# The recurrent mixer's three levels of scores as 32-column blocks in one group of matmuls

## The chip, the cores and the metric

The kernel runs on one core of a Trainium2 chip. The metric is device time in microseconds (us); one execution is one launch of the whole program. TensorE (PE in the profile) does the matmuls, its weight loads stand apart as PEld; VectorE is DVE, ScalarE is ACT, GpSimd is POOL, SyncE (SP) starts most transfers.

## The reference, cut to what matters

The reference is an encoder trunk of two layers over 1024 tokens of width 1024. Layer 0 mixes tokens by windowed attention, layer 1 by a gated linear recurrence that runs over the sequence in both directions; each mixer has four cross-attention heads beside it, and a ConvGLU follows each mixer. The change touches the recurrence alone:

```python
def gla_chunked(q, k, v, log_f):            # per head: 128 keys, 128 values
    b = jnp.cumsum(log_f, axis=2)           # within a chunk
    q_dec = q * jnp.exp(b)
    k_dec = k * jnp.exp(-b)
    s = jnp.where(causal, jnp.einsum('bcthk,bcshk->bchts', q_dec, k_dec), 0.0)
    o_intra = jnp.einsum('bchts,bcshv->bcthv', s, v)
    ...                                     # plus q_dec times a state carried from chunk to chunk
```

Scores `s` are wanted between tokens of one chunk, for the forward direction where the key is not later than the query, for the backward direction where it is not earlier.

## The kernel before, in words

The kernel works in chunks of 128 tokens. A call of `direction` handles one head `h`, one direction `d` and one half `b` of the sequence, so 512 tokens or four chunks; there are 8 heads x 2 directions x 2 halves = 32 such calls, in the order (0,0), (1,1), (0,1), (1,0) of (d, b) within a head. Everything in it is laid out as 128 keys (partitions) by 512 tokens.

**The scores of one call.** A bank of PSUM, `pa`, holds 4 chunks of 128 x 128 scores, the key's token on the partition and the query's token in the column. To keep the exponentials in range they are made at three levels:

- level 16: `E1` (queries) and `E2` (keys), scaled relative to the middle of each block of 32 tokens; L1116 multiplies them as one full 128 x 128 product for each chunk;
- level 32: one tile `G` whose earlier or later halves of 32 tokens hold scaled keys and scaled queries; L1136 multiplies, for each chunk, two blocks of 32 x 32 off the diagonal, over the product of level 16;
- level 64: a second `G`, and L1136 puts one block of 64 x 64 in each chunk.

Between the levels `step` (L1122, L1123) carries the decays `EP` and `ER` to the next block size; half of each `G` is made by POOL (L1130), half by DVE (L1131). Then a masked copy on DVE (L1146) takes only the wanted triangle out of `pa` into a zeroed tile `Az`, which goes to `As`. Beside it `ER` is transposed (`pt`, L1155), copied to `kT` by ACT (L1157) and multiplied with the values (`pu`, L1160) to carry the state.

**Buffers.** `E1`, `E2`, both `G`, and the four scratch tiles before them (`a_`, `L1`, `R`, `B`) rotate through five buffers with the tag `E`, eight allocations a call. So `L1` of the next call, written by the second activation (L1082), is put into the buffer of this call's `E1`, and may be written when the level-16 product has read it. `pa` rotates through two banks, which the cross-attention's scores `ps` share; `pt` has two banks, `pu`, `po` one each, and `pj`, the projections, two.

**What sets the order.** The projections of the next head (`proj`, three matmuls of 512 columns for each product: L81, L82, L83), the cross-attention units and the output products (`po`, L1184) are independent work that fills TensorE between the steps of a call. Nobody writes that order out: a scheduler runs the program against its own table of costs when it is built and fixes the order of each engine's queue. On the chip each queue then runs strictly in that order and waits for semaphores. `issue_after(x)` forbids the scheduler to place the instructions under it ahead of `x`.

The float32 matmuls that aren't split into high and low parts (`pa`, `pu`, `po`) appear in the trace as two passes each, with a weight load for each pass: the 128 matmuls of L1116 are 256 rows. A transpose is one pass.

Of the kernel before, what the change touches and what calls it, by code (L numbers as in the profile page):

```python
# [6 lines left out]
F32 = mybir.dt.float32  # L7
# [9 lines left out]
P = 128  # L17
# [29 lines left out]
def build(tc, A, out):  # L47
    nc = tc.nc
    act, dve, pool, pe = nc.scalar, nc.vector, nc.gpsimd, nc.tensor
# [889 lines left out]
    def hgrn():  # L939
# [5 lines left out]
        V, G = [late.tile([P, 3, NT, P], F32, name=x) for x in ("v", "gs")]  # L945
        wp = tc.alloc_tile_pool(name="hg1", bufs=1, side="right", reuse_waits="tile")
        psp = tc.alloc_tile_pool(name="hgps", bufs=1, space=PSUM, side="right", reuse_waits="tile")
        psj = tc.alloc_tile_pool(name="hgpj", bufs=2, space=PSUM, reuse_waits="tile")
        PB = dict(pa=2, pt=2, pu=1, po=1)

        def bank(tag, shape=(P, 4, P)):
            return psp.tile(list(shape), F32, tag=tag, bufs=PB[tag], name=tag)

        class Bank:
            tile = staticmethod(lambda shape, dt, tag, bufs, name: psp.tile(shape, dt, tag=tag, bufs=bufs, name=name))

        tags = {"pj": ("pj", 2, psj), "ps": ("pa", 2, Bank), "pt": ("pt", 2, Bank), "po": [lambda x=x: bank(x, (P, 512)) for x in ("po", "pu")], "sm": 1, "xo": "ot"}
        one = lambda shape, name, dt=F32: wp.tile(shape, dt, bufs=1, name=name)
        for x in PB:
            bank(x)  # L960
        lg = one([P, 2, 2, 8], "lg")
        nc.sync.dma_start(lg, A["lb_logits"])
        bng = one([P, 8], "bng")
# [102 lines left out]
        def direction(h, r, d, b, qin, S, As):  # L1066
# [3 lines left out]
            lt, er = (0, 1) if d else (1, 0)  # L1070

            def E():
                return early.tile([P, 512], F32, tag="E", bufs=5, name="E")

            def halves(x, n):
                x = x.rearrange("p (b a c) -> p b a c", a=2, c=n)
                return x[:, :, lt, :], x[:, :, er, :]
# [16 lines left out]
            ER = early.tile([P, 512], F32, tag="ER", bufs=2, name="ER")  # L1094
            act.activation(EP, B, AF.Exp)
            act.activation(ER, R, AF.Exp)
            pa = bank("pa")
            E1, E2 = E(), E()
            Bl, Be = halves(B, 16)
            Rl, Re = halves(R, 16)  # L1100
# [3 lines left out]
            def parts(n):  # L1104
                return halves(EP, n) + halves(ER, n) + halves(q, n) + halves(k, n)
# [5 lines left out]
            dve.tensor_tensor(e2, re_, ke, op=ALU.mult)  # L1111
            dve.tensor_tensor(e1, e1, qe, op=ALU.mult)
            dve.tensor_tensor(l2, l2, kl, op=ALU.mult)
            for c in range(4):
                cs = slice(c * P, (c + 1) * P)
                pe.matmul(pa[:, c, :], E2[:, cs], E1[:, cs], start=True, stop=True)  # L1116

            def step(n):
                pl_, pe_, rl_, re_ = parts(n)[:4]
                e = 0 if d else n - 1  # L1120
                nb = 512 // (2 * n)
                dve.tensor_tensor(re_, re_, bc(pl_[:, :, e:e + 1], [P, nb, n]), op=ALU.mult)  # L1122
                dve.tensor_tensor(pl_, pl_, bc(pe_[:, :, e:e + 1], [P, nb, n]), op=ALU.mult)  # L1123

            for n in (32, 64):
                step(n // 2)
                G = E()
                gl, ge = halves(G, n)
                pl_, pe_, rl_, re_, ql, qe, kl, ke = parts(n)
                pool.tensor_tensor(gl, pl_, ql, op=ALU.mult)  # L1130
                dve.tensor_tensor(ge, re_, ke, op=ALU.mult)  # L1131
                for c in range(4):
                    for i in range(64 // n):
                        o = i * 2 * n
                        lo, eo = o + lt * n, o + er * n
                        pe.matmul(pa[eo:eo + n, c, lo:lo + n], G[:, c * P + eo:c * P + eo + n],  # L1136
                                  G[:, c * P + lo:c * P + lo + n], start=True, stop=True,
                                  tile_position=(0, eo))
            step(64)
            dec = wp.tile([P, 4], F32, tag="dec", bufs=2, name="dec")  # L1140
            e = 0 if d else P - 1
# [16 lines left out]
            pu = bank("pu")  # L1158
# [54 lines left out]
        def head(h, r):  # L1213
            qin = [wp.tile([P, T], F32, tag=f"qin{d}", bufs=1, name="qin") for d in range(2)]
            S = [wp.tile([P, NT, P], F32, tag=f"S{d}", bufs=1, name="S") for d in range(2)]
            As = [None, None]
            for i, (d, b) in enumerate(((0, 0), (1, 1), (0, 1), (1, 0))):
                direction(h, r, d, b, qin[d], S[d], As)
                if i < len(r["later"]):
                    r["run"](r["later"][i])  # L1220
                cross(HX[h][i])
                if h == 7 and i == 2:
                    wo1.early(psj, 2, es)
            if h == 7:
                early.release()
                es.release()
                eq.release()
                wo1.open(2, 0)
            for i, b in enumerate((1, 0)):
                output(h, r, b, qin, S, As)  # L1230
                cross(HX[h][4 + i])
# [44 lines left out]
    wo0.finish()  # L1276
    ffn(0, wo0, h2d, True, (0, 1), (0, 1))
    hgrn()
    wo1.finish()
    ffn(1, wo1, out, False, (1, 0), (1, 0))  # L1280
# [83 lines left out]
```

## Time and profile before

| what | value |
|---|---|
| median of 3 runs (lowest to highest) | 2722.17 us (2719.72 to 2722.46) |
| span of the profiled execution, first to last instruction | 2718.9 us |
| TensorE busy over the span | 2656.1 us (98%) |
| DVE, ACT, POOL busy | 1830.8, 1396.6, 472.8 us |
| mean granted clock of TensorE | 0.993 |
| recurrent stage | about 1250 to 1950 us of the span |

How to read it: a row of the timeline gives the start, the time from the first start to the last end, and `xN` passes merged. Matmuls overlap in the pipeline, so what a matmul costs is read from the distance between starts, not from its own duration. In a shape such as `128*32` the second number is how many columns of the array the instruction uses, and `128x32` is the output columns that it streams.

### The profile page before, as it was taken

What the parts mean: (1) busy time and instruction counts of PE and PEld (TensorE: products, weight loads), DVE (VectorE), ACT (ScalarE), POOL (GpSimd) and SP (SyncE); (2) the same over time, 40 slices, a digit from 0 to 9 for tenths busy, and PEclk for the clock granted to TensorE, in tenths of its full rate; (3) what the DMA queues carried; (4) which work ended last, traced back from release to release, by engine and by line L of the source; (5) the groups of instructions that cost most, each with busy time, mean ns of one, the idle gap of its engine ahead of it and who ended that gap; (6) DMA issues with size and microseconds to landing.
All of it is one profiled execution on the core that took longest, in us unless ns stands there. A gap on an engine that the chain in (4) does not pass through costs nothing.

```text
span 2718.9 us, 37473 instructions
## 1 busy us (share of the span) xinstructions
PE 2656.1 (98%) x13472; PEld 2228.1 (82%) x13472; DVE 1830.8 (67%) x3040; ACT 1396.6 (51%) x2556; POOL 472.8 (17%) x520
## 2 busy tenths in 40 slices
PE   8899999999999999999999999999999999999998
PEld 7888897788888887887888888888788788888887
DVE  6487787678565655478686777868567756566447
ACT  6367667545444444454444545545454544444443
POOL 1231110211111100032232231312121111110003
PEclk9899999999999999999999999999999999999999
DMA  7674213667777757573234541111466787775766
GB/s 283 204 167 101 59 37 113 183 192 182 205 198 199 201 149 259 191 250 132 80 131 113 117 93 55 44 54 37 124 213 178 187 212 200 203 198 153 233 195 233
DMA packets 215307, 432.12 MB, mean 159 GB/s; under 512 B 20560, under 2 KB 77264, under 8 KB 209488
## 3 DMA queue, kind: packets, MB, share of 16 engines
q1 hardware_dynamic: 188128, 335.07, 38.3%
q0 software_dynamic: 24544, 90.19, 16.0%
q10 hardware_dynamic: 2448, 4.46, 0.5%
q8 instruction: 106, 1.74, 0.3%
q14 instruction: 81, 0.66, 0.1%
HBM read 335.79 MB, written 117.96 MB: 167 GB/s over the span
## 4 chain that ended last, share of the span: by engine, by line
PE 89%; DVE 6%; ACT 2%; DMA 2%; issue 1%; SPq 0%; POOL 0%; DVEq 0%; POOLq 0%; ACTq 0%
PE X L535 29%; PE V L535 11%; PE pj L81 8%; PE pj L82 7%; PE pj L83 7%; PE Y L535 5%; PE pb L81 3%; PE pb L82 3%; PE pb L83 3%; PE po L1184 1%; PE pa L1136 1%; PE pt L116 1%; PE pt L338 1%; PE pa L1116 1%; PE pu L1160 1%
## 5 line engine op out<-in xcount | busy, mean ns | idle before, releaser
L87 DVE TENSOR_TENSOR wl<-st,wh 128x1024 fp32r<-128x1024 f32 (+1 forms) x238 | 262.2, 1109 | 326.7 <-ACT wh L86 323.0
L86 ACT CAST wh<-st 128x1024 fp32r<-128x1024 f32 (+1 forms) x238 | 222.5, 937 | 295.4 <-PE X L535 195.9
L81 PE MATMUL pj<-uh,wh 128*128 128x512 f32 x512 | 206.9, 404 | 6.6 <-DVE xl L87 4.6
L535 PE MATMUL X<-wl,wh 128*128 128x512 f32 x528 | 204.7, 389 | 0.0
L535 PE MATMUL X<-wh,wl 128*128 128x512 f32 x528 | 204.6, 389 | 0.0
L82 PE MATMUL pj<-ul,wh 128*128 128x512 f32 x512 | 203.2, 397 | 0.1
L83 PE MATMUL pj<-uh,wl 128*128 128x512 f32 x512 | 203.2, 397 | 0.0
L535 PE MATMUL X<-wh 128*128 128x512 f32 x528 | 198.8, 390 | 1.3 <-ACT c L908 1.3
L81 PE MATMUL pj<-wh,uh 128*128 128x384 f32 (+1 forms) x512 | 191.4, 374 | 0.0
L82 PE MATMUL pj<-wl,uh 128*128 128x384 f32 (+1 forms) x512 | 187.5, 366 | 0.0
L83 PE MATMUL pj<-wh,ul 128*128 128x384 f32 (+1 forms) x512 | 187.1, 365 | 0.0
L535 PE MATMUL V<-uh,wh 128*128 128x512 f32 x344 | 133.8, 389 | 0.0
L535 PE MATMUL V<-ul,wh 128*128 128x512 f32 x344 | 133.8, 389 | 0.0
L535 PE MATMUL V<-uh,wl 128*128 128x512 f32 x344 | 133.8, 389 | 0.0
L77 DVE TENSOR_TENSOR wl<-st,wh 128x1024 fp32r<-128x1024 f32 (+1 forms) x92 | 113.3, 1239 | 27.1 <-ACT wh L76 26.2
L76 ACT CAST wh<-st 128x1024 fp32r<-128x1024 f32 (+1 forms) x99 | 99.8, 1014 | 47.1 <-PE pj L82 27.2
L81 PEld LDWEIGHTS pj<-uh,wh 128*128 128x128 f32 x512 | 97.2, 190 | 26.9 <-DVE xl L87 5.5
L1130 POOL TENSOR_TENSOR E<-EP,q 128x256 f32<-128x256 f32 x64 | 54.6, 854 | 371.6 <-DVE EP L1123 286.5
L535 PEld LDWEIGHTS X<-wh 128*128 128x128 f32 x528 | 99.1, 188 | 22.7 <-ACT c L908 1.7
L535 PEld LDWEIGHTS X<-wh,wl 128*128 128x128 f32 x528 | 99.1, 188 | 20.7
L535 PEld LDWEIGHTS X<-wl,wh 128*128 128x128 f32 x528 | 99.1, 188 | 20.4
L83 PEld LDWEIGHTS pj<-uh,wl 128*128 128x128 f32 x512 | 97.4, 190 | 19.7
(348 smaller groups left out, 7336.1 us busy)
## 6 DMA issues: line engine op xcount, KB each, us to landing
st<-hid SPq DMA_DIRECT2D x154, 256.0 KB, 3.2
st<-in_ffw_dram SPq DMA_DIRECT2D x108, 256.0 KB, 3.3
w2s<-in_ffw_dram POOLq DMA_DIRECT2D x24, 1024.0 KB, 7.9
st<-in_ffw_dram SPq DMA_DIRECT2D x46, 512.0 KB, 3.8
hid<-tt SPq DMA_DIRECT2D x88, 256.0 KB, 4.7
st<-w2s SPq DMA_DIRECT2D x88, 256.0 KB, 3.2
sx<-in_ffw_dram SPq DMA_DIRECT2D x84, 256.0 KB, 4.0
sy<-in_ffw_dram SPq DMA_DIRECT2D x42, 512.0 KB, 6.0
```

The costliest lines, as they stand in the source:

```text
L76: act.copy(h[:, :n], raw)
L77: (eng or dve).tensor_tensor(l[:, :n], raw, h[:, :n].bitcast(F32), op=ALU.subtract)
L81: pe.matmul(o, ah, bh, start=first, stop=False)
L82: pe.matmul(o, ah, bl, start=False, stop=False)
L83: pe.matmul(o, al, bh, start=False, stop=last)
L86: act.copy(h, src)
L87: dve.tensor_tensor(l, src, h.bitcast(F32), op=ALU.subtract)
L116: pe.transpose(ps[:, k, :], u[:, (4 * b + k) * P:(4 * b + k + 1) * P], ident)
L338: pe.transpose(tp[:, j, :], sm[:, j, c * P:(c + 1) * P], ident)
L535: pe.matmul(o, x, y, start=new, stop=e, skip_group_check=not first)
L1116: pe.matmul(pa[:, c, :], E2[:, cs], E1[:, cs], start=True, stop=True)
L1130: pool.tensor_tensor(gl, pl_, ql, op=ALU.mult)
```

## The change

All three levels are cut so that each matmul uses 32 columns of the array: level 16 as the four 32 x 32 blocks on the diagonal of each chunk (it was one 128 x 128 product), level 32 as before, level 64 as two blocks of 32 x 64 for each chunk (it was one of 64 x 64). They are issued as one group behind the operand of the last level: first the eight blocks of level 64, then, held back by `issue_after`, the sixteen of level 16 and the eight of level 32. That is 32 matmuls a call where there were 4 + 8 + 4 = 16, over the whole kernel 1024 for 512.

Since the blocks don't cover the bank, `pa` is now one bank for each direction, set to zero once by DVE at the start of the mixer. The cross-attention's `ps` moves from the tag `pa` to the two banks of `pt`.

```diff
-        PB = dict(pa=2, pt=2, pu=1, po=1)
+        PB = dict(pt=2, pu=1, po=1)
...
-        tags = {"pj": ("pj", 2, psj), "ps": ("pa", 2, Bank), "pt": ("pt", 2, Bank), "po": [lambda x=x: bank(x, (P, 512)) for x in ("po", "pu")], "sm": 1, "xo": "ot"}
+        tags = {"pj": ("pj", 2, psj), "ps": ("pt", 2, Bank), "pt": ("pt", 2, Bank), "po": [lambda x=x: bank(x, (P, 512)) for x in ("po", "pu")], "sm": 1, "xo": "ot"}
...
+        PA = [psp.tile([P, 4, P], F32, tag=f"pa{d}", bufs=1, name="pa") for d in range(2)]
+        for x in PA:
+            dve.memset(x, 0.0)
...
-            pa = bank("pa")
+            pa = PA[d]
...
-            for c in range(4):
-                cs = slice(c * P, (c + 1) * P)
-                pe.matmul(pa[:, c, :], E2[:, cs], E1[:, cs], start=True, stop=True)
+            def block(c, i, j, x, y, n=32):
+
+                return pe.matmul(pa[i:i + 32, c, j:j + n], x[:, c * P + i:c * P + i + 32], y[:, c * P + j:c * P + j + n],
+                                 start=True, stop=True, tile_position=(0, i))
...
+                if n == 32:
+                    G32 = G
+            for c in range(4):
+                for o in (0, 32):
+                    mm = block(c, er * 64 + o, lt * 64, G, G, 64)
+            with tc.issue_after(mm.ins):
                 for c in range(4):
-                    for i in range(64 // n):
-                        o = i * 2 * n
-                        lo, eo = o + lt * n, o + er * n
-                        pe.matmul(pa[eo:eo + n, c, lo:lo + n], G[:, c * P + eo:c * P + eo + n],
-                                  G[:, c * P + lo:c * P + lo + n], start=True, stop=True,
-                                  tile_position=(0, eo))
+                    for o in range(0, P, 32):
+                        block(c, o, o, E2, E1)
+                for c in range(4):
+                    for o in (0, 64):
+                        block(c, o + er * 32, o + lt * 32, G32, G32)
```

In the changed file the lines of a call stand further down: `block` is L1119, the transposes of `ER` L1164, the state's product L1169, the output product L1193.

The order of the queues moves with it. TensorE, the fourth call of the first head, before: a call's scores between the state's product `pu` and the projections `pj`.

```order
L1160 MATMUL pu<-v,kT 128x128 x4
L1116 MATMUL pa<-E 128x128 x4
L1136 MATMUL pa<-E 32x32 x8
L1136 MATMUL pa<-E 64x64 x4
L83 MATMUL pj<-uh,wl 128x512
L81 MATMUL pj<-uh,wh 128x512
```

The fourth call of the first head now: `32x64` is level 64, the 24 blocks of `32x32` are levels 16 and 32.

```order
L1193 MATMUL po<-S,qin 128x128
L1119 MATMUL pa<-E 32x64 x8
L1119 MATMUL pa<-E 32x32 x24
L1164 MATMUL pt<-ident,ER 128x128 x4
L81 MATMUL pj<-uh,wh 128x512
L82 MATMUL pj<-ul,wh 128x512
```

Three shapes of the array in a row have become one. Counted over the whole queue, 32-column runs between other work are 73 now (19 calls have all 32 matmuls together, the other 13 are still cut into pieces); before, there were 82 runs of 32 or 64 columns, 57 of them entered from a 128-column matmul and 25 that are a 64-column run right behind a 32-column run.

TensorE, the second call of the second head, before: behind the scores come two projections, the transposes of `ER`, and 24 more projections ahead of the product `pu`.

```order
L1116 MATMUL pa<-E 128x128 x4
L1136 MATMUL pa<-E 32x32 x8
L1136 MATMUL pa<-E 64x64 x4
L83 MATMUL pj<-uh,wl 128x512
L81 MATMUL pj<-uh,wh 128x512
L1155 MATMUL pt<-ident,ER 128x128 x4
L82 MATMUL pj<-ul,wh 128x512
L83 MATMUL pj<-uh,wl 128x512
```

The same call now: the transposes, two projections, `pu`, and then 24 projections (the first three are shown) up to the next call's group.

```order
L1119 MATMUL pa<-E 32x64 x8
L1119 MATMUL pa<-E 32x32 x24
L1164 MATMUL pt<-ident,ER 128x128 x4
L82 MATMUL pj<-ul,wh 128x512
L83 MATMUL pj<-uh,wl 128x512
L1169 MATMUL pu<-v,kT 128x128 x4
L81 MATMUL pj<-uh,wh 128x512
L82 MATMUL pj<-ul,wh 128x512
L83 MATMUL pj<-uh,wl 128x512
```

The level-16 product, whose end lets the next call's L1082 start, has moved from ahead of the call's other scores to behind the level-64 blocks, and between it and the next call's first block stands only the work of these rows. Outside the recurrent stage TensorE's order is the same as before.

## The prediction

> **What bounds the kernel now.** I read the page's totals and chain first, then the busy times of the stage that changes, then what TensorE waits for in it.
>
> ```profile
> span 2718.9 us, 37473 instructions
> ...
> PE 2656.1 (98%) x13472; PEld 2228.1 (82%) x13472; DVE 1830.8 (67%) x3040; ACT 1396.6 (51%) x2556; POOL 472.8 (17%) x520
> ...
> PE 89%; DVE 6%; ACT 2%; DMA 2%; issue 1%; SPq 0%; POOL 0%; DVEq 0%; POOLq 0%; ACTq 0%
> ```
>
> ```profile
> 1250.00:1950.00 700.00, 688.00 (x4177) 576.34 (x4176) 521.37 (x1039) 352.95 (x771) 176.28 (x189) 1.00 0.29 83
> ```
>
> ```profile
> PE pj L81 <- DVE xl L87: 2.1, 1, 2.1
> PE po L1184 <- DVE S L1169: 2.1, 1, 2.1
> PE pt L217 <- DVE xp L212: 0.9, 2, 0.8
> PE pa L1116 <- ACT xp L208: 0.9, 2, 0.5
> ```
>
> TensorE is 98% busy and holds 89% of the chain that ended last. In the recurrent stage (columns: stretch, length, PE, PEld, DVE, ACT, POOL, then the granted clock, here 1.00) it is busy 688 of 700 us, DVE 521. The longest waits of TensorE there are about 2 us, and those for the scores under 1. So a microsecond that TensorE's queue loses here is one that the kernel loses, as long as no new wait takes its place.
>
> **What the scores cost on TensorE.** The rows grouped by shape, in the same stretch:
>
> ```profile
> L1116 PE MATMUL pa<-E 128*128 128x128 f32 x256 | 35.7, 276 | 1.3 <-ACT xp L208 0.9 <-DVE E L1113 0.3
> L1136 PE MATMUL pa<-E 128*64 128x64 f32 x256 | 22.6, 229 | 0.0
> L1136 PE MATMUL pa<-E 128*32 128x32 f32 x512 | 17.4, 200 | 0.0
> ```
>
> These durations overlap, so I don't add them; I take the distances of starts. One call in one piece, between projections:
>
> ```profile
> 1556.65 0.39 PE L83 MATMUL pj<-uh,wl 128*128 128x512 f32 x1
> 1556.88 1.05 PE L1116 MATMUL pa<-E 128*128 128x128 f32 x8
> 1557.86 1.05 PE L1136 MATMUL pa<-E 128*32 128x32 f32 x24
> 1558.85 0.50 PE L81 MATMUL pj<-uh,wh 128*128 128x512 f32 x1
> 1559.18 0.39 PE L82 MATMUL pj<-ul,wh 128*128 128x512 f32 x1
> 1559.41 0.40 PE L83 MATMUL pj<-uh,wl 128*128 128x512 f32 x1
> ```
>
> A projection takes 0.23 (1559.18 to 1559.41). From 1556.88 to 1559.18 are 2.30, with one projection in it: the call's scores cost **2.07 us**. The second L1136 row merges 16 passes of 32 columns and 8 of 64. The 32-column passes can be taken apart with four other places:
>
> ```profile
> 1277.20 0.39 PE L83 MATMUL pj<-uh,wl 128*128 128x512 f32 x1
> 1277.52 0.31 PE L1136 MATMUL pa<-E 128*32 128x32 f32 x6
> 1277.76 0.50 PE L81 MATMUL pj<-wh,uh 128*128 128x512 f32 x1
> 1278.10 0.39 PE L82 MATMUL pj<-wl,uh 128*128 128x512 f32 x1
> ...
> 1309.41 0.26 PE L1136 MATMUL pa<-E 128*32 128x32 f32 x4
> 1309.59 0.50 PE L81 MATMUL pj<-wh,uh 128*128 128x512 f32 x1
> ...
> 1397.83 0.45 PE L1136 MATMUL pa<-E 128*32 128x32 f32 x16
> 1398.20 0.50 PE L81 MATMUL pj<-uh,wh 128*128 128x512 f32 x1
> ...
> 1440.85 0.25 PE L1136 MATMUL pa<-E 128*32 128x32 f32 x2
> 1441.03 0.50 PE L81 MATMUL pj<-wh,uh 128*128 128x512 f32 x1
> ```
>
> From a run's start to the next start: one matmul (2 passes) 0.18, two 0.18, three 0.24, eight 0.37. The second matmul is free: it goes to another 32 columns of the array than the first (64 apart) and runs beside it. The third, alone with its columns, costs 0.06; two more pairs and a partner cost the rest. So a matmul of 32 x 32 occupies its 32 columns for 0.064 us, and two such column groups overlap fully: 0.032 a matmul, 0.016 a pass. Next, the price of changing shape: from 1277.20 to 1278.10 are 0.90, less two projections 0.44, less the bodies 0.064 + 0.064: **0.32 us for each run of narrow matmuls**, in and out. And the 64-column part: 0.99 (1557.86 to 1558.85) less 0.37 is 0.62, less the 0.12 that a run has beyond its body (0.37 - 8 x 0.032) 0.50, or 0.125 for each matmul that streams 64 columns.
>
> **Before, all calls:** 32 x 2.07 = 66.2. The queue has 57 runs entered from a wide matmul instead of 32, 25 x 0.32 = 8.0 more, and seven calls have no direct step from 32 to 64 columns, 7 x 0.12 = 0.8 less. Sum **73.4 us**.
>
> **Now, a call:** level 64: eight matmuls of 32 x 64 in two column groups, four rounds of 0.125 = 0.50, if neighbouring groups overlap as those 64 apart do. Level 32: eight of 32 x 32 in two groups, 0.26, as before. Level 16: sixteen over four groups. With four side by side 0.26, with two 0.51. No row shows four; I take 0.30, near the lower end, because the second group added less than 0.01 in the rows above. Entry and exit 0.32. Sum 1.38, times 32 is 44.2. There are 73 runs instead of 32: 41 x 0.32 = 13.1. Sum **57.3**, with level 16's ends 56.0 to 64.0. TensorE gains **16.1 us** (9.4 to 17.4).
>
> [...]
>
> **What is late next.** The level-16 product now ends last, and L1082 of the next call waits for its buffer. One call after such a release, to its last level-64 operand:
>
> ```profile
> 1545.34 0.63 ACT L1082 ACTIVATE E<-E 128x512 f32<-128x512 f32 x1
> ...
> 1555.26 0.76 POOL L1130 TENSOR_TENSOR E<-EP,q 128x256 f32<-128x256 f32 x1 [1.21 <-DVE EP L1123]
> ```
>
> ```profile
> 1471.66 0.63 ACT L1082 ACTIVATE E<-E 128x512 f32<-128x512 f32 x1 [4.23 <-PE pa L1116]
> ...
> 1486.91 0.79 POOL L1130 TENSOR_TENSOR E<-EP,q 128x256 f32<-128x256 f32 x1 [1.88 <-DVE EP L1123]
> ```
>
> The chain takes 10.7 us in the first, 16.0 in the second, where other work stands between its steps on ACT and DVE. Against that I hold the TensorE work that the new order puts from the end of level 16 to the next call's first block, priced by the distances above (a pass of 128 columns 0.11: eight in 1556.88 to 1557.86). It is 12.0 us or more at 30 of 31 places, 12.0 to 13.0 at twelve, and 15.9 at the call of the second row. One place is short, the second call of the second head: level 32 0.26, four transposes 0.44, 26 projections 5.9, `pu` 0.9, changes of shape 0.2: 7.7 us. There TensorE stands for 10.7 - 7.7 = **3 us**. At the other places the cover is over 1 us and I take 0.
>
> **The rest.** The two memsets on DVE, no row before:
>
> ```profile
> L988 POOL MEMSET Az<- 128x512 f32 x2 | 1.0, 526 | 0.0
> L1146 DVE COPY_PREDICATED Az<-gm,pa 128x512 f32<-128x512 uint8 x32 | 23.6, 736 | 7.7 <-PE pa L1136 7.5
> ```
>
> 0 to 1.5 us (two at 0.74); they lie under the first head's projections, 87 matmuls or 20 us ahead of the first score, so 0. The masked copy now waits for the whole group: it waited 7.5 us in all, behind it the next call's DVE steps; at most 0.8 us more (1.38 - 0.62) at the seven places where it already waits, 5 us; DVE has 179 us idle in the stage, so 0. The banks of `ps` come from `pt`, eight units: nothing if a transpose's bank is free, 0.9 each (row of L217 above) if not, 7 us; the order is built around it, so 0. Some of the 12 us that TensorE stands now may go, some come; 0, with 3 either way.
>
> **Sum.** 2718.9 - 16.1 + 3 = 2705.8 for the profiled execution, which lies 3.3 under the median of 2722.17: predicted **2709 us**.
>
> **The rivals.**
>
> *Two groups at a time.* Level 16 takes 0.51: 6.7 us more, 2716. For: two is all that the rows show. Against: nothing in them shows a limit.
>
> *A long train is fed too slowly.* The longest train of narrow passes so far is 24; now it is 64, and the queue ahead of TensorE may run dry. The gain is gone where 32 x (x + 0.32) + 13.1 = 73.4, so x = 1.56 us for 64 passes, 0.024 a pass. If all but the first 16 go at the mean of the 24-pass train, 0.99 / 24 = 0.041, a call takes 0.25 + 1.97 + 0.32 = 2.54, and the kernel 2746. Against: 16 passes at 0.016 without a sign of slowing. [...]
>
> *Neighbours don't overlap.* Level 64 now pairs adjacent column groups, which no row shows. If neighbours go one after the other, level 64 takes 1.00 and level 16 0.51: 0.71 x 32 = 23 more, 2732. With no overlap but that of level 32, level 16 takes 1.02: 2748.
>
> *The buffer of level 16 becomes the bound* (slower). The place is L1082, held until the group's end; the price is the chain less the cover. With a chain c everywhere the twelve places at about 12.7 and the short one eat the gain of 16.1 when 12 (c - 12.7) + (c - 7.7) = 16.1, c = 13.6. At c = 15 they take 35 us, 2741. For: 16.0 in the row above. Against: where the chain was that long, the new order has put 15.9 us of cover.
>
> *It doesn't do what it says.* One group a call is not what the queue has: 13 of 32 calls are still in pieces. That is in the sum (41 runs).
>
> **How the numbers follow.** Forecast 0.55 (2699 to 2713); two groups 0.13; slow feed 0.07; neighbours 0.10; the buffer 0.15, spread from 2715 up. The range of eight in ten is **2699 to 2732**: below, 2709 less 1.3 (level 16's end), 3 (no stall), 3 (old waits gone) and rounding; above, adjacent groups in turn. Past it lie half of the last two cases, the worst of the feed and a little below. A measurement of this kernel can tell about 0.2%, 5.4 us, from no change. Faster than 2716.7: the forecast and most of the two-group case, **0.65**. Within: the rest of that case, half of the slow feed, part of the buffer, **0.17**. Slower than 2727.6: neighbours, most of the buffer, half of the feed, **0.18**.
>
> **What would show it.** In the new profile: a whole group about 1.2 us from its first start to the start of what follows; 32-column passes of level 16 at 8 to 10 ns each; TensorE idle about 3 us ahead of one group in the second head; the stage some 13 us shorter. Wrong if a group takes over 2 us, or if TensorE waits at many groups for POOL or DVE.

## The result, and the profile after

The changed kernel takes **2718.07 us** (median of 12 runs, 2714.51 to 2723.15), the kernel before 2719.59 us on the same chips (median of 12, 2717.62 to 2722.88): ratio **0.9994**, 95% interval 0.9985 to 1.0002. It is no faster by any amount that the measurement can tell. The forecast was 2709.

First the page's totals, then the whole recurrent stage in one row for each kernel, from the same matmul to the same matmul. Columns: stretch, its length, then busy us (and instructions) of PE, PEld, DVE, ACT and POOL, then the granted clock, the DMA share and GB/s. Before:

```profile
1134.70:2056.10 921.40, 909.40 (x5193) 760.26 (x5192) 668.91 (x1239) 470.85 (x972) 230.16 (x234) 1.00 0.38 114
```

After:

```profile
span 2714.1 us, 39502 instructions
...
PE 2638.7 (97%) x14496; PEld 2204.5 (81%) x14496; DVE 1828.5 (67%) x3042; ACT 1391.6 (51%) x2556; POOL 468.4 (17%) x520
```

```profile
1131.60:2050.60 919.00, 896.70 (x6218) 740.83 (x6217) 665.39 (x1241) 466.58 (x972) 226.41 (x234) 0.99 0.38 115
```

The profiled span is 4.8 us shorter, but 3.1 of that lie ahead of the stage, where the programs are alike (it begins at 1131.6 for 1134.7), and 0.7 are lost behind it: the scatter of an execution. The stage itself is 2.4 us shorter: TensorE is busy 12.7 us less (909.4 to 896.7) and stands 10.3 us more (12.0 to 22.3). And the clock column says 0.99 where it said 1.00. That is no accident of the two profiles: the granted clock is 0.9914 on average over the 12 runs of the changed kernel, 0.9935 over 26 runs of the kernel before (those beside old_places), which is some 5.6 us more lost over the span.

**The group itself is as forecast.** TensorE at one of the cross units, after:

```profile
1660.09 0.39 PE L83 MATMUL pj<-uh,wl 128*128 128x512 f32 x1
1660.41 1.17 PE L1119 MATMUL pa<-E 128*32 128x64 f32 x64
1661.51 0.66 PE L1164 MATMUL pt<-ident,ER 128*128 128x128 f32 x4
1661.92 0.36 PE L81 MATMUL ps<-kvh,xh 128*128 128x256 f32 x1
...
1663.00 0.28 PE L83 MATMUL ps<-kvh,xl 128*128 128x256 f32 x1
1664.73 1.16 PE L1169 MATMUL pu<-v,kT 128*128 128x128 f32 x8 [1.45 <-ACT kT L1166]
1665.65 0.36 PE L81 MATMUL ps<-kvh,xh 128*128 128x256 f32 x1
```

All 64 passes of a call go in 1.10 us from first start to next start (1660.41 to 1661.51), where 1.2 was forecast. The last three rows show a new wait, to which the next part returns.

**Where TensorE stands now.** Five stretches of the stage, after:

```profile
1385.00:1410.00 25.00, 20.89 (x219) 16.90 (x218) 22.96 (x43) 13.76 (x25) 8.59 (x10) 1.00 0.46 153
...
1490.00:1500.00 10.00, 6.91 (x94) 5.68 (x93) 6.55 (x12) 6.49 (x15) 4.80 (x5) 0.86 0.83 190
...
1660.00:1670.00 10.00, 8.41 (x107) 6.98 (x106) 7.88 (x14) 7.38 (x16) 2.82 (x3) 1.00 0.06 20
...
1826.00:1832.00 6.00, 4.38 (x84) 3.47 (x83) 3.87 (x7) 4.29 (x9) 3.09 (x3) 0.98 0.20 74
...
1895.00:1947.00 52.00, 42.59 (x329) 33.88 (x327) 36.37 (x81) 24.07 (x65) 11.48 (x12) 0.90 0.38 114
```

The same places before; of the three cross units only one stood:

```profile
1390.00:1415.00 25.00, 23.64 (x162) 19.60 (x161) 24.10 (x45) 13.31 (x24) 8.54 (x11) 1.00 0.43 153
...
1835.00:1845.00 10.00, 7.86 (x40) 6.42 (x39) 9.90 (x24) 6.78 (x17) 1.06 (x2) 0.87 0.12 43
...
1900.00:1952.00 52.00, 45.77 (x296) 37.62 (x295) 37.59 (x84) 24.12 (x65) 11.42 (x12) 0.97 0.36 112
```

The second head: 4.1 us of idle for 1.4; here are two of its three waits.

```profile
1390.70 1.13 PE L1169 MATMUL pu<-v,kT 128*128 128x128 f32 x8 [0.97 <-DVE S L1178]
...
1398.98 1.17 PE L1119 MATMUL pa<-E 128*32 128x64 f32 x64 [1.44 <-DVE s L1041]
```

The second is the group that the prediction named: its last operand, POOL's half of `G`, is written from 1398.18 to 1398.93, though the label names `s`. The third wait, 1.7 for `q`, stood before too, with 1.4.

Three cross units: 3.1 + 1.6 + 1.6 = 6.3 for 2.1. The last head: 9.4 for 6.2. That is 10.1 of the 10.3. The waits by name, after (total us, times, longest):

```profile
PE pu L1169 <- ACT kT L1166: 4.4, 3, 1.5
PE pu L1169 <- ACT xo L223: 2.3, 1, 2.3
PE pb L81 <- ACT oh L86: 2.0, 2, 1.3
PE pb L83 <- DVE oe L87: 1.9, 1, 1.9
```

The first row was in no list of before. The others are steps of the last head, where few projections are left to lie over a wait.

**The second price of idle.** What follows the wait at 1494.78, after, by 2 us and then TensorE's rows:

```profile
1494.00:1496.00 2.00, 0.86 (x5) 0.66 (x5) 1.29 (x3) 2.00 (x5) 1.12 (x1) 1.00 0.92 188
1496.00:1498.00 2.00, 1.48 (x10) 1.48 (x11) 2.00 (x5) 1.70 (x3) 0.15 (x1) 0.81 1.01 201
1498.00:1500.00 2.00, 2.00 (x9) 1.81 (x9) 2.00 (x4) 1.59 (x6) 0.00 (x0) 0.50 0.96 197
1500.00:1502.00 2.00, 2.00 (x9) 1.61 (x8) 2.00 (x6) 1.19 (x3) 0.00 (x0) 0.83 1.10 229
```

```profile
1499.03 0.63 PE L81 MATMUL pj<-uh,wh 128*128 128x512 f32 x1
1499.46 0.63 PE L82 MATMUL pj<-ul,wh 128*128 128x512 f32 x1
1499.88 0.63 PE L83 MATMUL pj<-uh,wl 128*128 128x512 f32 x1
```

The granted clock falls to one half, and projections start 0.42 us apart, not 0.23 as at full clock. Such a stretch costs (0.19 + 0.50 + 0.17) x 2 = 1.7 us, and in it TensorE counts as busy. The stage before holds two, at 1842 and 1941, 3.4 us; after it holds five, at 1497, 1831, 1903 and two from 1930, 8.5 us.

So I count the stage in three parts: idle, the loss in half-clock stretches (sum of 1 - clock over windows of 1 us), and the rest, **work at full clock**. Before: 12.0 + 3.4 + 906.0. After: 22.3 + 8.5 + 888.2. TensorE was spared **17.8 us** of work, and 10.3 + 5.1 came back.

### The profile page after: what moved, and what is told of

Its sections match the earlier page's. It is cut to its first block, busy times and chain, and to the rows that moved or that the text cites. A ratio compares the mean times of both kernels' runs of the same rounds, so it can differ in the third digit from the quotient of the medians.

```text
span 2714.1 us, 39502 instructions
## 1 busy us (share of the span) xinstructions
PE 2638.7 (97%) x14496; PEld 2204.5 (81%) x14496; DVE 1828.5 (67%) x3042; ACT 1391.6 (51%) x2556; POOL 468.4 (17%) x520
## 5 line engine op out<-in xcount | busy, mean ns | idle before, releaser
L87 DVE TENSOR_TENSOR wl<-st,wh 128x1024 fp32r<-128x1024 f32 (+1 forms) x238 | 262.6, 1110 | 326.7 <-ACT wh L86 321.6
L77 DVE TENSOR_TENSOR wl<-st,wh 128x1024 fp32r<-128x1024 f32 (+1 forms) x92 | 119.0, 1301 | 23.3 <-ACT wh L76 22.8
```

The lines of the kernel that those rows point to most:

```text
L77: (eng or dve).tensor_tensor(l[:, :n], raw, h[:, :n].bitcast(F32), op=ALU.subtract)
L87: dve.tensor_tensor(l, src, h.bitcast(F32), op=ALU.subtract)
```

## The experiments

Twelve more kernels, each timed beside the kernel before (4 to 11 times). "Runs" counts how many pieces the 32- and 64-column matmuls form in TensorE's queue, between matmuls of the full width.

| kernel | us, median | ratio to before, 95% interval | runs | stage | idle | half clock | work |
|---|---|---|---|---|---|---|---|
| before | 2719.59 | 1 | 57 | 921.4 | 12.0 | 3.4 | 906.0 |
| after | 2718.07 | 0.9994 (0.9985 to 1.0002) | 73 | 919.0 | 22.3 | 8.5 | 888.2 |
| ps_back | 2712.76 | 0.9971 (0.9960 to 0.9982) | 66 | 914.7 | 21.6 | 5.1 | 888.0 |
| hold_free | 2737.19 | 1.0062 (1.0048 to 1.0076) | 75 | 938.6 | 36.6 | 15.4 | 886.6 |
| group_pri | 2703.25 | 0.9935 (0.9923 to 0.9947) | 32 | 899.5 | 20.5 | 3.4 | 875.6 |
| before_ps | 2724.40 | 1.0015 (1.0007 to 1.0024) | 60 | 924.6 | 15.6 | 3.4 | 905.6 |
| old_places | 2718.90 | 0.9996 (0.9987 to 1.0005) | 79 | 919.7 | 22.9 | 6.8 | 890.0 |
| old_pri | 2713.76 | 0.9978 (0.9970 to 0.9987) | 49 | 916.7 | 31.3 | 3.4 | 882.0 |
| before_pri | 2712.73 | 0.9975 (0.9966 to 0.9984) | 43 | 915.5 | 11.4 | 5.1 | 899.0 |
| pri_ps | 2694.91 | 0.9911 (0.9896 to 0.9926) | 32 | 892.7 | 15.1 | 5.1 | 872.5 |
| before_no16 | 2699.97 | 0.9927 (0.9914 to 0.9939) | 69 | 901.4 | 11.1 | 3.4 | 886.9 |
| after_pad | 2731.24 | 1.0044 (1.0030 to 1.0057) | 81 | 932.9 | 18.8 | 10.2 | 903.9 |
| blocks_only | 2726.45 | 1.0028 (1.0016 to 1.0040) | 82 | 927.4 | 27.7 | 10.3 | 889.4 |
| before_hold | 2744.47 | 1.0090 (1.0077 to 1.0104) | 77 | 944.2 | 21.3 | 10.2 | 912.6 |

The right half is of one profiled execution each, the left half of all runs; the granted clock moves between runs of one kernel (0.990 to 0.992 for the changed one, some 5 us), so half clock does too. How far idle and work vary from one execution to the next no second profile of a kernel shows. Every edit also gives the scheduler a new order for the whole stage; where that decides a verdict I say so.

**ps_back: the cross scores back in the score banks.**

```diff
+        last = [0]
+        class Scores:
+            def tile(*a, **k):
+                last[0] = 1 - last[0]
+                return PA[last[0]].rearrange("p c t -> p (c t)").rearrange("p (a b) -> p a b", a=2)
-        tags = {"pj": ("pj", 2, psj), "ps": ("pt", 2, Bank), "pt": ("pt", 2, Bank), "po": [lambda x=x: bank(x, (P, 512)) for x in ("po", "pu")], "sm": 1, "xo": "ot"}
+        tags = {"pj": ("pj", 2, psj), "ps": ("pa", 2, Scores), "pt": ("pt", 2, Bank), "po": [lambda x=x: bank(x, (P, 512)) for x in ("po", "pu")], "sm": 1, "xo": "ot"}
...
             pa = PA[d]
+            last[0] = d
```

> The changed kernel, but the cross scores (ps) again share the two score banks pa, as before the change; pt serves transposes alone. In the changed kernel's stage of 919.0 us TensorE idles 22.3 us (12.0 before) and loses 8.5 us to half-clock stretches that follow idle places (3.4 before). Theory 'ps banks': the transposes' bank is taken by ps, so pu waits for kT between two ps groups (three places of 1.45 us, one of 1.3); with ps moved back these waits go, idle falls by 5 to 7 us to 15 to 17, one or two half-clock stretches (1.7 us each) go with them, and the time falls to about 2709. Theory 'held buffers': idle stays at 20 to 24 and the time falls only by the 7 fewer broken runs of narrow matmuls that this order has (66 for 73, 0.32 us each, 2.2 us), about 2716.

Measured: 5.3 us faster than the changed kernel, idle 21.6, half clock 5.1 for 8.5. The same cross unit as above, in this kernel:

```profile
1666.92 0.66 PE L1172 MATMUL pt<-ident,ER 128*128 128x128 f32 x4
1667.50 0.39 PE L81 MATMUL pa<-kvh,xh 128*128 128x256 f32 x1
...
1669.58 0.28 PE L83 MATMUL pa<-kvh,xl 128*128 128x256 f32 x1
1670.55 1.16 PE L1177 MATMUL pu<-v,kT 128*128 128x128 f32 x8 [0.69 <-ACT kT L1174]
```

In the changed kernel the transposes of `ER` and the first `ps` fill both banks of `pt`, and the program gives the second `ps` the transposes' bank. It can't start before the copy to `kT` has emptied that, so it stands behind `pu`, which needs the same copy. Here twelve matmuls for `ps` stand ahead of `pu` where there were six, and the wait is 0.69 for 1.45. The bank is only half of that wait, though. In the kernel before six matmuls for `ps` stood behind `pu` as well, and `pu` did not wait, because 17 projections stood between the transposes and `pu`. Before:

```profile
1660.65 0.66 PE L1155 MATMUL pt<-ident,ER 128*128 128x128 f32 x4
...
1665.77 1.05 PE L1160 MATMUL pu<-v,kT 128*128 128x128 f32 x8
1666.57 0.36 PE L81 MATMUL ps<-kvh,xh 128*128 128x256 f32 x1
```

In the new order none stands there. The shorter wait is shown; the whole idle is not, since it falls by 0.7 only: other waits came with this order (the first `ps` of one cross unit waits 2.5 for `kvh` in place of 1.3). The time lies midway between the two theories (2709 and 2716), the idle where the other theory put it; of the 4.3 us by which the stage is shorter, 3.4 are half clock. The run decides for neither.

**before_ps: the same edit the other way, alone.**

```diff
-        tags = {"pj": ("pj", 2, psj), "ps": ("pa", 2, Bank), "pt": ("pt", 2, Bank), "po": [lambda x=x: bank(x, (P, 512)) for x in ("po", "pu")], "sm": 1, "xo": "ot"}
+        tags = {"pj": ("pj", 2, psj), "ps": ("pt", 2, Bank), "pt": ("pt", 2, Bank), "po": [lambda x=x: bank(x, (P, 512)) for x in ("po", "pu")], "sm": 1, "xo": "ot"}
```

> The kernel before with one edit, the cross scores (ps) moved from the score banks to the transposes' banks pt, as the change does. Theory 'ps banks': TensorE idles 5 to 7 us more than the 12.0 of before, with one or two more half-clock stretches of 1.7 us, time about 2725 to 2728. Theory 'held buffers': within 2 us of before, 2718 to 2722 (60 runs of narrow matmuls for 57, 1 us).

Measured: 4.3 us slower than the before runs of its comparison (2720.13), idle 15.6, work 0.4 lower. The direction of "ps banks" and a little less than its size; the ends of the interval are 2 and 6.5 us. But it isn't the wait of the changed kernel. Its wait for the copy:

```profile
PE pu L1160 <- ACT kT L1157: 0.2, 1, 0.2
```

What grew are waits of projections for `q`, 4.8 us for 1.7. So moving `ps` costs some 4 to 5 us in these two pairs of kernels, by different waits; blocks_only below goes the other way.

**group_pri: the groups whole.**

```diff
+            with tc.high_priority(AHEAD):
                 for c in range(4):
                     for o in (0, 32):
                         mm = block(c, er * 64 + o, lt * 64, G, G, 64)
                 with tc.issue_after(mm.ins):
...
```

> The changed kernel with a higher priority for the group of score matmuls, so that all 32 groups stand unbroken in TensorE's queue (32 runs of narrow matmuls for 73). Theory 'broken groups' (the gain is lost because 41 extra entries and exits cost 0.32 us each): busy time falls by about 13 us, idle stays near 22, time about 2705. Theory 'the pieces were fillers' (a piece of a group was what TensorE ran while something else was late): busy falls by 13 but idle grows by 8 to 13, time 2713 to 2718.

Measured: 14.8 us faster than the changed kernel. The whole stage:

```profile
1137.80:2037.30 899.50, 879.05 (x6218) 734.89 (x6217) 674.42 (x1242) 471.56 (x972) 226.39 (x234) 1.00 0.39 117
```

Work falls by 12.6 us for 41 entries fewer, 0.31 each; idle stays (20.5). "Broken groups" is shown, "the pieces were fillers" is refuted. This loss was in the forecast's sum; what it shows is that it need not have been there.

**before_pri: priority alone.**

```diff
+            with tc.high_priority(AHEAD):
                 for c in range(4):
                     cs = slice(c * P, (c + 1) * P)
                     pe.matmul(pa[:, c, :], E2[:, cs], E1[:, cs], start=True, stop=True)
...
+                with tc.high_priority(AHEAD):
                     for c in range(4):
                         for i in range(64 // n):
...
```

> The kernel before with a higher priority for its score matmuls and nothing else (no blocks, no hold, ps in the score banks): 43 runs of narrow matmuls for 57, level 16's products in 32 unbroken fours for 42 pieces. Theory 'an entry and exit costs 0.32 us wherever it stands': work at full clock falls from 906.0 by 14 x 0.32 = 4.5 us, time about 2715. Theory 'priority helps in some other way (fewer waits)': idle falls below the 12.0 of before and the time below 2711; 'the pieces were fillers': idle grows by 4 or more, time at or above 2719.

Measured: 6.9 us faster than before, work 7.0 lower (4.5 expected), idle 11.4. Priority gives the kernel before its entries back, and no waits with them. What the other 2.5 us of work are is open; level 16's products stand in fewer pieces too (32 for 42).

**pri_ps: both edits together.** group_pri's and ps_back's.

> group_pri and ps_back together: unbroken groups and the cross scores in the score banks. If the two causes are separate, ps_back's 5 us come on top of group_pri's 2703.25: about 2698 to 2700. If both only move the same waits, 2702 to 2706.

Measured: 2694.91, 23.2 us below the changed kernel and 8.3 below group_pri. The stage:

```profile
1133.20:2025.90 892.70, 877.64 (x6217) 734.77 (x6217) 676.61 (x1241) 468.73 (x972) 225.14 (x234) 0.99 0.39 118
```

In this pair of edits the gains add up: 23.2 for 14.8 + 5.3, with an interval of about 4 us either way. No wait for `kT` is left, here or in group_pri, which has `ps` in the transposes' banks. Against before_pri, which has the priority and `ps` in the score banks as well, the time is 17.8 us lower for 26.5 us less work; in the two profiles idle takes 3.7 of that back, and the profiled run is the fastest of this kernel. This version is 0.9% faster than the kernel before (0.74 to 1.04), and by about as much faster than the changed one.

**hold_free: no early step of the next call in a held buffer.**

```diff
-            a_, L1 = E(), E()
+            EP = early.tile([P, 512], F32, tag="EP", bufs=2, name="EP")
+            ER = early.tile([P, 512], F32, tag="ER", bufs=2, name="ER")
+            a_, L1 = E(), EP
...
-            R, B = E(), E()
+            R, B = ER, a_
...
             act.activation(e1, Re, AF.Exp, scale=-1.0)
+            act.activation(ER, R, AF.Exp)
```

> The changed kernel, but a call takes 5 operand buffers instead of 8: the first logarithm is written into the tile EP, R into the tile ER, and the scan is done in place, so that no early step of the next call uses a buffer that level 16's held operands occupy. One activation of level 16 (0.4 us) moves ahead of the exponential of R. Theory 'held buffers': the next call's chain no longer waits for the group, idle of TensorE falls from 22.3 to about 12 to 15, time about 2708 to 2710. Theory 'ps banks' or 'scheduler order': idle stays at 20 or more, time 2716 to 2720 (75 broken runs for 73).

Measured: 19 us slower, which neither theory expected. Its waits between 1550 and 1580:

```profile
PE pt L1164 <- ACT ot L1205: 6.7, 1, 6.7
ACT ot L1205 <- DMA oT<-xo: 6.5, 1, 6.5
```

With its buffers free the next call's chain moved forward in the order, and the output's single tile `ot` came to wait for the store of its last contents, at the head of ACT's queue, with TensorE behind it. This measures another wait than the one meant. It says nothing of the hold; the next run does.

**old_places: no hold.**

```diff
+            for c in range(4):
+                for o in range(0, P, 32):
+                    block(c, o, o, E2, E1)
...
                 if n == 32:
                     G32 = G
+                    for c in range(4):
+                        for o in (0, 64):
+                            block(c, o + er * 32, o + lt * 32, G32, G32)
...
-            with tc.issue_after(mm.ins):
-                for c in range(4):
-                    for o in range(0, P, 32):
-                        block(c, o, o, E2, E1)
-                for c in range(4):
-                    for o in (0, 64):
-                        block(c, o + er * 32, o + lt * 32, G32, G32)
```

> The changed kernel's blocks and zeroed banks, but each level's matmuls stand where they stood before: level 16 behind its own operands, level 32 behind its own, level 64 last; nothing is held back. In TensorE's queue they make 79 runs of narrow matmuls (73 in the changed kernel, 57 before), so its work at full clock should be 888.2 + 6 x 0.32 = 890 us. Theory 'held operands' (the group holds level 16's buffers, the next call's chain starts late, and TensorE stands): idle falls from 22.3 to about 12 to 14, half-clock loss to about 3.4, time about 2707. Theory 'the hold costs TensorE nothing': idle stays at 20 or more, time 2716 to 2721.

Measured: 2718.90, idle 22.9, work 890.0. Work came to the tenth; the idle did not move. "Held operands" is refuted as the cause of the changed kernel's idle, although its trace shows ACT waiting at that buffer (17 times for 30.7 us, after):

```profile
ACT E L1085 <- PE pa L1119: 30.7, 17, 7.4
```

ACT is busy half of the stage (466.6 of 919.0 us, after), and could wait there without TensorE.

**old_pri: no hold, each level whole.** old_places with each level's matmuls under `tc.high_priority(AHEAD)`.

> The same blocks at their old places, each level with a higher priority: 49 unbroken runs of narrow matmuls, against 32 in group_pri (2703.25 us, idle 20.5, work at full clock 875.6). Work: 875.6 + 17 x 0.32 = 881. Theory 'held operands': idle falls from 20.5 to about 12, time about 2700. Theory 'the hold costs TensorE nothing': idle stays at 18 to 22, time about 2707 to 2709, so one group a call is the better of the two by its fewer entries.

Measured: 2713.76, work 882.0 (881 expected), idle 31.3 for group_pri's 20.5. A level at its old place under priority can reach its operand too early:

```profile
PE pa L1119 <- POOL E L1139: 5.1, 8, 1.3
```

In group_pri, with the hold:

```profile
PE pa L1119 <- POOL E L1134: 4.3, 4, 1.6
```

With two smaller rows the scores wait 8.0 here for 4.3 there; the other 7 us of the difference stand at other steps (`gs`, `ot`, `S`, `on`). Neither theory has this. In this pair the hold goes with less idle, not with more.

**before_no16: less work, nothing of the change's order.** It leaves out level 16's product for three of four chunks.

```diff
-            for c in range(4):
+            for c in range(1):
                 cs = slice(c * P, (c + 1) * P)
                 pe.matmul(pa[:, c, :], E2[:, cs], E1[:, cs], start=True, stop=True)
```

(with the two zeroed banks, and `ps` in them as in ps_back.)

> The kernel before with less for TensorE to do and nothing of the change's order: level 16's product is left out for three of the four chunks of each call (the output lacks these scores), the two score banks are fixed and zeroed as in the change, ps stays in them. 32 x 6 passes of 128 columns at 0.11 are 21.1 us less; the queue has 69 runs of narrow matmuls for 57, 3.8 us more: work at full clock 906.0 - 17.3 = 888.7, the changed kernel's 888.2. Theory 'less cover' (the chains on DVE and ACT take as long as before, so a TensorE that is done 17 us sooner stands at their ends, whatever made it faster): idle rises from 12.0 to 18 or more, the time falls by 5 to 12 us, to 2708 to 2715. Theory 'the change's own waits' (its order, its banks): idle stays within 3 of 12, time about 2700 to 2704.

Measured: 19.7 us faster than before, work 19.1 lower, idle 11.1:

```profile
1136.90:2038.30 901.40, 890.28 (x5002) 740.17 (x5001) 665.62 (x1242) 467.54 (x972) 230.66 (x234) 1.00 0.38 117
```

A TensorE with as little work as in the changed kernel doesn't stand more: every microsecond spared is kept. "Less cover" by itself is refuted as the cause.

**after_pad: work put back.** Level 64 of each group is done twice.

```diff
+            for _ in range(2):
                 for c in range(4):
                     for o in (0, 32):
                         mm = block(c, er * 64 + o, lt * 64, G, G, 64)
```

> The changed kernel with the level-64 part of each group done twice: 32 x 0.50 = 16.0 us more work for TensorE, and 81 runs of narrow matmuls for 73, 2.6 us more; work at full clock 888.2 + 18.6 = 906.8, that of the kernel before (906.0). Theory 'less cover': the added work lies where TensorE stood; idle falls from 22.3 to 12 to 16 with one to three half-clock stretches fewer, time 2722 to 2729, at least 8 us less than the added work would give. Theory 'the change's own waits': idle stays at 20 or more, time about 2735.

Measured: 13.2 us slower than the changed kernel for 15.7 us of work; idle 3.5 lower, half clock 1.7 higher. Both the time and the idle lie between the two theories' numbers, so the run decides for neither; 84% of the added work is paid for.

**blocks_only: neither hold nor moved `ps`.** old_places with ps_back's banks.

> Of the change only the blocks and the zeroed banks: each level's matmuls at their old places (as in old_places) and the cross scores in the score banks (as in ps_back). 82 runs of narrow matmuls for the changed kernel's 73: work at full clock 888.2 + 9 x 0.32 = 891. old_places and ps_back each left idle at 22 to 23. Theory 'two causes, either enough' (the hold and the moved ps each bring waits of their own, and taking one away leaves the other's): with both gone idle falls to 11 to 14, time about 2705 to 2709. Theory 'a new order costs what it costs' (idle comes with any regrouping of the matmuls, whatever the buffers): idle 19 or more, time about 2714 to 2719.

Measured: 2726.45, idle 27.7. With both suspects gone the idle is larger. The kernel is 13.7 us slower than ps_back, which has the hold, and 7.5 us slower than old_places, which has `ps` in the transposes' banks: here moving `ps` back costs time. TensorE's largest wait, in the cross units:

```profile
PE pj L81 <- DVE xl L87: 8.9, 3, 4.7
```

This is a projection that waits for `xl`, a step of DVE; neither a score bank nor a score operand is in it.

**before_hold: the hold alone.**

```diff
+            mm = level(64, G, range(1))
+            with tc.issue_after(mm.ins):
+                for c in range(4):
+                    cs = slice(c * P, (c + 1) * P)
+                    pe.matmul(pa[:, c, :], E2[:, cs], E1[:, cs], start=True, stop=True)
+                level(32, G32)
+                level(64, G)
```

(`level` holds the matmuls that stood in the loop; they are taken out of it.)

> The kernel before with the hold alone: its own matmuls, level 16 still as products of 128 columns, but all three levels of a call issued behind the last level's operand (behind one more matmul of level 64, whose result is overwritten); ps in the score banks, no zeroed banks. 77 runs of narrow matmuls for 57 and 32 extra matmuls: work at full clock 906.0 + 6.4 + 1.9 = 914. Theory 'the hold brings waits of its own': idle rises from 12.0 to 17 or more, with half-clock stretches behind it, time 2735 or more. Theory 'the hold costs TensorE nothing': idle 10 to 14, time about 2726 to 2730.

Measured: 24.3 us slower than its before (2720.15); work 912.6, idle 21.3, half clock 10.2. In the kernel before, the hold does bring waits, and again the largest is at `xl`, not at a score:

```profile
PE pj L81 <- DVE xl L87: 10.1, 3, 3.5
```

Together with old_places and blocks_only: the hold costs 16 us of standing and half clock here, costs nothing in the changed kernel, and saves in the kernel with `ps` back. It has no price of its own; what has one is the order that comes out.

## Why the prediction was wrong in its sum

The range held the time, the likeliest case did not come: no change that can be told had been given 0.17. That the time lies in the range is luck, because none of the rivals that widened the range came true.

- *Before 73.4, now 57.3, gain 16.1:* right. Work at full clock fell by 17.8. Between before_pri and pri_ps, with priority on both sides, it fell by 26.5, where these prices give 25.6 (32 x 0.69 + 11 x 0.32).
- *A call's group 1.38 us; four column groups side by side 0.26:* right. The group takes 1.10 from start to start, and the sixteen blocks' rows show a train of 16 passes over four column groups (seven of its eight matmuls are of level 16, in the program's order) in 0.26, where 1397.83 of before showed 0.37 over two. No run shows the 4 us by which the forecast's own case reaches above 2709, to 2713. After:

```profile
1291.69 0.33 PE L1119 MATMUL pa<-E 128*32 128x32 f32 x16
1291.95 0.50 PE L81 MATMUL pj<-wh,uh 128*128 128x512 f32 x1
```

- *Rivals "two groups at a time", "fed too slowly", "neighbours don't overlap":* refuted by the same rows. 64 passes in 1.10 us are 0.017 a pass, over 64 passes on end in alternating column groups. The half of the slow feed that the chances put at no change that can be told rests on no row or run.
- *0.32 us for each run:* right, 0.31 by group_pri (the working as written, 0.90 - 0.44 - 0.128, gives 0.33). But the 41 extra runs were taken as given; a priority removes them.
- *A stall of 3 us in the second head:* right in place, near in size. The chain from the second activation (L1085 now, at 1388.33) to POOL's last operand takes 10.6 for the 10.7 forecast; TensorE stands 2.4 in it, 1.0 ahead of `pu` and 1.4 ahead of the group.
- *"At the other places the cover is over 1 us and I take 0":* right for what it speaks of, and too narrow. No other score waits for its operand. The last head, whose order also moved, stands 3.2 us more.
- *The banks of `ps`, "nothing if a transpose's bank is free, 0.9 each if not, 7 us; the order is built around it, so 0":* **this failed in part.** The 0.9 was misread: the row gives 0.9 for two waits, 0.45 each. The second `ps` stands behind `pu`, and so behind the copy, and no projection covers the copy any more; cross units stand 4.2 us more. But no fixed price hangs on the banks: with `ps` in the score banks the time is lower by 5.3 (ps_back), 4.3 (before against before_ps) and 8.3 (pri_ps against group_pri), and higher by 7.5 in blocks_only against old_places.
- *"Some of the 12 us that TensorE stands now may go, some come; 0, with 3 either way":* **this step failed**, in two ways. Idle rose by 10.3, of which the sum had 3, and no reason was given for the 0. And stretches of 3.4 us at half clock stand behind some of the waits (last section), which lose 8.5 us for 3.4 before: 5.1 us that the sum had no term for.
- *The masked copy and the memsets at 0:* right. DVE waits 2.5 us in all for the masked copy's bank, for 7.5; the memsets take 0.49 each, ahead of the stage's scores.
- *The buffer of level 16 becomes the bound:* ACT does wait there, TensorE doesn't suffer (old_places).

By the sum: 13.1 forecast, 2.4 measured in the stage. The 10.7 between them are idle beyond the 3 us (7.3) and half clock (5.1), less the 1.7 by which the work fell further.

**What stays open.** Fourteen orders of this stage stand 11 to 37 us. Those that keep the 128-column product of level 16 and no hold stand 11 to 16, the others 15 to 37, and no single part of the change takes the idle with it. That the scheduler's plan fits the matmuls of before better than the blocks would explain it; no run tests that. So where the time went is shown, why this order stands more is not.

## What to carry to other kernels

Price a change to an already dense stage in three parts: work that the bounding engine is spared, places where it will stand, and the half clock behind such places (here 8.5 us in the stage for 3.4 before); the first can be right to two microseconds and the sum still empty. A bank that is given away is not free because a scheduler can order around it: look at what it puts behind which copy, and what is left to cover that copy. Don't carry the price of such an edit from one order to another: here the same one went from 8.3 us won to 7.5 lost. And where an instruction's shape has a price of entry (here 0.31 us a run), count the pieces in the queue and give the group a priority before judging the idea: here 0.9994 became 0.9935 by the priority alone, and 0.9911 with `ps` moved back as well.

## What was not expected of the hardware

TensorE's granted clock fell to one half for 3.41 us (1.7 us lost) behind little idle, and the forecast had no term for it. After, at another cross unit:

```profile
1829.11 0.38 PE L82 MATMUL ps<-kvl,xh 128*128 128x256 f32 x1 [0.15 <-DVE kvl L87]
...
1831.43 1.79 PE L1169 MATMUL pu<-v,kT 128*128 128x128 f32 x8 [1.47 <-ACT kT L1166]
```

The fall came after 1.6 us of idle, in pieces of 0.15 and 1.47, while the wait of 1.45 ahead of 1664.73, in the same surroundings, brought none: the clock column says 1.00 from 1660 to 1670. Here are the half-clock stretches at 1497 and 1831, each with as long a stretch ahead of it:

```profile
1493.85:1497.26 3.41, 1.61 (x12) 1.40 (x12) 2.70 (x5) 3.41 (x8) 1.27 (x1) 1.00 0.93 185
1497.26:1500.67 3.41, 3.41 (x14) 3.09 (x14) 3.41 (x8) 2.65 (x7) 0.00 (x0) 0.50 0.97 199
...
1828.35:1831.77 3.42, 1.80 (x13) 1.40 (x13) 2.69 (x4) 3.42 (x7) 1.27 (x1) 1.00 0.00 0
1831.77:1835.18 3.41, 3.41 (x17) 3.22 (x16) 3.41 (x7) 2.71 (x8) 0.00 (x0) 0.50 0.01 2
```

TensorE stood 1.80 us in the 3.41 ahead of the first and 1.62 in the 3.42 ahead of the second. So in this execution two waits for `kT`, of 1.46 and 1.47 us, were followed by 1.7 us of loss each, and one of 1.45 by none. What decides between them is not shown.
